# A hand-ordered RWKV-7 recurrence: triangle stores in pieces from another queue, triangle loads from ScalarE, and norm and key copies at other places

## The chip, the cores and the metric

The kernel runs on one core of one Trainium2 chip. The metric is the device time of one execution in microseconds (us). The time of before is the median of three runs, 2522.64 us (2521.0 to 2528.43). The engines are PE (TensorE), DVE (VectorE), ACT (ScalarE), POOL (GpSimd) and SP (SyncE). SP only issues DMAs here; ACT issues DMAs too, in line with its own work: a DMA instruction that has to wait for something holds up whatever stands behind it on its engine.

## The reference

A two-layer trunk of width 1024: sliding-window attention, then RWKV-7 time mixing, for a prompt of 16 meta tokens and 2048 tokens, and for a sample of 8 sequences of 4 tokens. The change lies in the second layer's recurrence. For each of 16 heads a 64x64 state S is carried over the tokens:

```
def step(S, inp):
    r_t, w_t, k_t, v_t, a_t, b_t = inp
    sa = jnp.einsum('bhvk,bhk->bhv', S, a_t)
    S = S * w_t[:, :, None, :] + sa[..., None] * b_t[:, :, None, :] + v_t[..., None] * k_t[:, :, None, :]
    return S, jnp.einsum('bhvk,bhk->bhv', S, r_t)
```

After it y is normalised per head (mean and variance over 64), scaled and shifted by ln_g and ln_b, gets a bonus in v, is multiplied by a SiLU gate, projected by w_out and added to h; a last RMS norm gives the output.

## The kernel before

**Units and chunks.** The recurrence is the last phase, from about 1600 us to the end. It goes through units one after the other: unit 0 (meta tokens), units 1 to 16 (128 prompt tokens each, in four chunks of 32), and the sample. Within a chunk the 32 steps are solved at once. `chain` (L1417 on) writes a chunk: PE forms the right-hand side `C<-Z,L`, ACT copies it (`R0s<-C`), PE multiplies by the inverse of a triangular matrix (`C<-R0s,TT`), ACT copies the result into Z (`Z<-C`, four instructions), PE forms the state (`C<-Z,LS`), and DVE writes it into the next chunk's Z (`Z<-C,pe`, four). This chain is serial from chunk to chunk and from unit to unit.

**The triangles.** TT comes from work two units ahead. `scores` (called for the two halves of a unit) lets PE form `pz<-L,BK`, from which ACT copies the triangles into `LAs` (four instructions per half) and DVE masks the rest into L. `inverse` writes `LAs` to DRAM as `la_d` (two DMAs of 128 KB, by ACT, once both halves are there), loads that back in another layout as `LA` (two DMAs of 256 KB, by SP), multiplies it on POOL by `ln` (`LA<-LA,ln`), runs 31 elimination steps of two POOL instructions each (`XT<-LA,X` and `X<-X,XT`, on a tile X that starts as the constant `laneid`), multiplies by ln (`X<-X,ln`), and stores X as `tt_d` (SP, two DMAs). `load_TT` loads that as TT (SP, two DMAs), one unit before it is used. X and LA have two buffers each. `inverse` is a generator: where it yields, the caller puts other work in between.

**Beside it.** `keys` transposes BK on PE (`kt`), and ACT copies the result into LS in groups of four. `group_norm` is the norm of the previous unit: mean and variance on DVE (`mean<-Y`, `ytm<-Y,mean`, `var<-Y` from the squares `Y<-ytm` that ACT writes), a power on POOL (`var<-var,mhalf`), then `ytm<-ytm,var`, `,lng`, `,lnb` and `,vt` on DVE; the gate multiplies (`gt<-gt,pd`, `gt<-gt,ytm`), PE transposes it (`yps<-ident,gt`). The projections `pd<-wg,xg` and `po<-wo,yp` of earlier units are cut into pieces that fill PE while the chain waits.

**What sets the order.** For units 2 to 14, `steady` writes out by hand, chunk by chunk (`ch` 0 to 3), what stands where in each engine's queue. `run(norm)` advances the group norm to its end, `run(norm, to=MARK)` to its next mark, `next(...)` one yield; work inside `released()` is placed behind the chain's last instructions on each engine. `in_order()` pins the queues of DVE, ACT and POOL. PRE is 3: the first units are prepared before the steady part. `dma(out, in, s_)` issues from ACT, without the third argument from SP. A DMA signals one of eight semaphores, in turn, and waits for the DMA eight before to land.

Of the kernel before, what the change touches and what calls it, by code (L numbers as in the profile page):

```python
# [30 lines left out]
def tile_hybrid_step(ctx: ExitStack, tc: tile.TileContext, a, o, c):  # L31
# [877 lines left out]
    def load_vectors(u):  # L909

        u.BK, u.L = [], []
        if u.kind != "p":
            room = wl.tile([P, 2, 2 * KC * 64], F32, name="rooml", tag="L", bufs=nbuf["L"])
            u.spare = room[:, 1, 512:768].rearrange("p (g v) -> p g v", v=64)
            u.BKs = room[:, 1, 0:512].rearrange("p (h g c x) -> p h g c x", h=2, g=4, c=1)
        for half in range(2):
            hs = slice(half * 4, half * 4 + 4)
            BK = es.tile([P, 4, 4, 64], F32, name="BK", tag="BK", bufs=nbuf["BK"]) if u.kind == "p" else u.BKs[:, half]
            dma(BK, bk_d[u.blk][:, hs, u.c0:u.c0 + u.nch, :])
            u.BK.append(BK)  # L920
        for c2 in range(u.np):
            if u.kind == "p":
                L = wl.tile([P, 2, 2, KC, 64], F32, name="L", tag="L", bufs=nbuf["L"])
            else:
                L = room[:, 0].rearrange("p (e c g x) -> p e c g x", e=2, c=1, g=KC)
            u.L.append(L)
            w, c0 = min(2, u.nch - 2 * c2), u.c0 + 2 * c2
            for e, ps_ in HS:

                dma(L[ps_, e].rearrange("p c g x -> p (c g x)"), ar_d[u.blk][ps_, c0:c0 + w].rearrange("p c g x -> p (c g x)"))  # L930
            yield 0.8

    us = [begin(i, *x) for i, x in enumerate(units[:-1])]
# [14 lines left out]
    def scores(u, c2):  # L948
# [22 lines left out]
        for e in range(2):  # L971
            for cc in range(w):
                r0 = 64 * cc
                tt(v_, L[OS[e], e, cc], pss[e][r0:r0 + 64], mk[r0:r0 + 64, None, :].broadcast_to([64, KC, 64]), ALU.mult)

    def inverse(u, room=None, ln=None):

        nch = u.nch
        nl = nch * 16
        la_d = dramr.tile([2, nl // 2, 32, 32], F32, name="la_d", tag=f"la_d{nch}")  # L980
        u.tt_d = tt_d = dramr.tile([32, 4, 4 * nch * 32], F32, name="tt_d", tag=f"tt_d{nch}")
        for e in range(2):
            dma(la_d[e].rearrange("l j i -> j l i"),
                u.LAs[32 * e:32 * e + 32].rearrange("p h c g i -> p (h c g) i"), s_)
        yield
        eng = v_ if u.idx == 1 else g_
        if u.kind == "m":
            room = wl.tile([P, 2, 32 * 32], F32, name="roomm", tag="L", bufs=nbuf["L"])
        if room is not None:
            LA = room[:, 0].rearrange("p (j i) -> p j i", i=32)  # L990
            XX = room[:, 1].rearrange("p (a k i) -> p a k i", a=2, i=32)
        else:

            LA = wk.tile([P, 32, 32], F32, name="LA", tag="LA", bufs=2)
            XX = None
        if XX is None:
            X = wk.tile([P, 16, 32], F32, name="X", tag="X", bufs=2)
            XT = wk.tile([P, 16, 32], F32, name="XT", tag="XT")
        else:
            X, XT = XX[:, 0], XX[:, 1]  # L1000
        if ln is None:
            ln = wp.tile([P, 32], F32, name="ln", tag=("mu", "rst0")[u.idx % 2])
        if nch < 4:
            g_.memset(LA, 0.0)
            g_.memset(ln, 1.0)
        for hh in range(2):
            dma(LA[hh * 64:hh * 64 + nl], la_d.rearrange("e l j i -> (e l) j i"), s_ if u.idx < PRE else None)
            dma(ln[hh * 64:hh * 64 + nl], ln_d[u.idx].rearrange("q c g i -> (q c g) i"))
        tt(eng, LA, LA, ln.unsqueeze(2).broadcast_to([P, 32, 32]), ALU.mult)
        dma(X, c["laneid"])  # L1010

        low = 16 if u.kind == "m" else 0

        part = {2: 16}.get(u.idx, 0)
        cut = [(v_, 0, part), (g_, part, 16)] if 0 < part < 16 else [(v_, 0, 16)] if part else [(eng, 0, 16)]
        for j in range(low, 31):
            if j in (8, 16, 22, 26):
                yield
            w = 3 - j % 4 if u.kind == "s" else 31 - j
            for eng, k0, k1 in cut if w else ():  # L1020
                ks = slice(max(low // 2, k0), min(j // 2 + 1, k1))
                shape = [P, ks.stop - ks.start, w]
                if shape[1] <= 0:
                    continue
                tt(eng, XT[:, ks, :w], LA[:, j:j + 1, j + 1:j + 1 + w].broadcast_to(shape), X[:, ks, j:j + 1].broadcast_to(shape), ALU.mult)
                tt(eng, X[:, ks, j + 1:j + 1 + w], X[:, ks, j + 1:j + 1 + w], XT[:, ks, :w], ALU.add)
        for eng, k0, k1 in reversed(cut):
            u.inverted = tt(eng, X[:, k0:k1], X[:, k0:k1], ln[:, None, :].broadcast_to([P, k1 - k0, 32]), ALU.mult)
        for hh in range(2):
            dma(tt_d[hh:32:2].rearrange("k q (l i) -> (q l) k i", i=32), X[hh * 64:hh * 64 + nl])  # L1030
# [11 lines left out]
    with ExitStack() as ph:  # L1042
# [144 lines left out]
        for x, b in enumerate(order):  # L1187
# [39 lines left out]
            if follow is None:  # L1227

                if delay:
                    todo.append((b, prv))  # L1230
                    rest_v = rest_values()
                    fill(rest_v, V0)
                wrx.close()
                es = wrx.enter_context(tc.tile_pool(name="es", bufs=1, side="right", reuse_waits="tile"))
                wl = wrx.enter_context(tc.tile_pool(name="wl", bufs=1, side="right", reuse_waits="tile"))
                for u in us[:PRE]:
                    for _ in load_vectors(u):
                        pass
                if nblk > 2:
                    banks = lambda u: [pd.tile([P, KC, 64], F32, name="pz", tag="pd") for _ in range(2)]  # L1240
                    las = wk.tile([P, 2048], F32, name="las", tag="dx", bufs=1)
                    room1 = wk.tile([P, 2, 1024], F32, name="room1", tag="xn", bufs=1)
                    for i, x0, room in ((1, 0, room1), (0, 1024, None)):
                        u = us[i]
                        u.LAs = las[:64, x0:x0 + 256 * u.nch].rearrange("p (h c g i) -> p h c g i", h=2, g=4, i=32)
                        for c2 in range(u.np):
                            all_of(scores(u, c2))
                        for _ in inverse(u, room, las[:, x0 + 1024 - 32:x0 + 1024] if i == 0 else las[:, 1536:1568]):
                            pass
            if follow is not None:  # L1250
# [18 lines left out]
    with ExitStack() as ph:  # L1269
# [71 lines left out]
        def elementwise(u):  # L1341
            load = idle() if u.L else load_vectors(u)
            next(load, None)
            small_loads(u)
            if u.tt_d is None:
                new_LAs(u)
                for c2 in range(u.np):
                    all_of(scores(u, c2))
                    next(load, None)
                    yield 0.8  # L1350
                for _ in inverse(u):
                    pass
            load_TT(u)
            yield 0.8
# [22 lines left out]
        def keys(u, c2):  # L1377
# [13 lines left out]
            for half, ps in enumerate(pss):  # L1391
                hs = slice(half * 4, half * 4 + 4)
                for cc in range(w):
                    for e in range(2):
                        act(u.LS[c2][cc][OS[e], e, hs, :], ps[cc * 64:cc * 64 + 64, :, e, :])

        def solve(u, ch, Z, R0s, out):

# [371 lines left out]
        def steady(i, u, pe):  # L1770
# [9 lines left out]
            for ch in range(4):  # L1780
# [4 lines left out]

                left = rests[::-1]
                del rests[:]
                if ch == 3:
                    run(norm)
                with released():  # L1790
                    if ch == 2:
                        next(inv.get(i + 1, idle()), None)
# [19 lines left out]
                        run(gen)  # L1812
                if ch == 2:
                    with released():
                        inv[s.idx] = inverse(s)
                        next(inv[s.idx])
                        all_of(sc)
                run(pe[ch], 1.2)
                next(rec)
                with released():  # L1820
                    if ch == 0:
# [2 lines left out]
                        first = L0s.pop(s.idx, None)  # L1824
                        load_BK(s)
                        s.L.append(first or load_L(s, 0))
                        all_of(kt)
                    if ch == 3:
                        all_of(kt)
                        next(inv[s.idx])  # L1830
                    else:
                        next(inv.get(i + 1, idle()), None)
                if ch < 2:
                    run(norm, to=MARK)
                elif ch == 3:
                    run(norms_[u.idx], to=MARK)
                run(pe[ch], 1.9)
                next(rec, None)
                with released():
# [3 lines left out]
                    if ch == 2 and i + 1 in inv:  # L1843
                        load_TT(us[i + 1])
                if ch == 2:
                    norms_[u.idx] = group_norm(u)
                    run(norms_[u.idx], to=MARK)
                    if ch == 3 and i + 3 < len(us):
# [4 lines left out]
                if ch == 1:  # L1853
                    with released():
                        new_LAs(s)
                        all_of(scores(s, 0))
                rests.append(pe[ch])
                for part in PLAN.get((i, ch), ()):
                    with released():
# [214 lines left out]
```

## Time and profile before

| | |
|---|---|
| median of the runs (2521.0, 2522.64, 2528.43) | 2522.64 us |
| the profiled execution's own time | 2526.93 us |
| its span | 2525.2 us |
| granted clock, mean over the span | 0.958 |
| busy: PE, DVE, ACT, POOL | 2238.5, 1666.3, 1169.9, 1035.9 us |
| instructions | 60868 |

The profiled execution is one run; its numbers are compared with its own time, 2526.93. In groups of instructions, the columns are busy us, the mean duration in ns, then the idle time of the engine just ahead of that group and what ended it. In a timeline a row is start, duration, engine, operation and tiles, and in brackets the idle time ahead and its releaser. Rows with an engine name ending in q (SPq, ACTq) are DMA issues: their duration is the issue, not the transfer. In the chain of waits a row that begins with DMA gives the time from issue to landing.

### The profile page before, as it was taken

What the parts mean: (1) busy time and instruction counts of PE and PEld (TensorE: products, weight loads), DVE (VectorE), ACT (ScalarE), POOL (GpSimd) and SP (SyncE); (2) the same over time, 40 slices, a digit from 0 to 9 for tenths busy, and PEclk for the clock granted to TensorE, in tenths of its full rate; (3) what the DMA queues carried; (4) which work ended last, traced back from release to release, by engine and by line L of the source; (5) the groups of instructions that cost most, each with busy time, mean ns of one, the idle gap of its engine ahead of it and who ended that gap; (6) DMA issues with size and microseconds to landing.
All of it is one profiled execution on the core that took longest, in us unless ns stands there. A gap on an engine that the chain in (4) does not pass through costs nothing. (4 is left out here: it accounts for less than half of the span.)

```text
span 2525.2 us, 60868 instructions
## 1 busy us (share of the span) xinstructions
PE 2238.5 (89%) x24932; PEld 1539.7 (61%) x24932; DVE 1666.3 (66%) x3181; ACT 1169.9 (46%) x2799; POOL 1035.9 (41%) x1572
## 2 busy tenths in 40 slices
PE   6989989899989897899999999666898888888897
PEld 5877768677855445577776668444555555555553
DVE  6586674577656987866556656555666666666674
ACT  6675465566432433554343444333444444445431
POOL 4242132333111334543333334314776766767613
PEclk9999999999999998899999999777999999999998
DMA  9433122333247564432222222575555655655323
GB/s 207 126 105 108 64 80 80 112 99 100 98 130 224 198 223 164 138 85 89 96 85 93 98 81 92 162 199 156 130 122 143 147 122 143 144 130 155 94 61 75
DMA packets 346234, 312.98 MB, mean 124 GB/s; under 512 B 205546, under 2 KB 282218, under 8 KB 344131
## 3 DMA queue, kind: packets, MB, share of 16 engines
q1 hardware_dynamic: 302515, 286.15, 38.4%
q10 hardware_dynamic: 41824, 19.15, 3.6%
q0 software_dynamic: 1616, 3.79, 0.7%
q8 instruction: 196, 3.21, 0.5%
q14 instruction: 83, 0.68, 0.1%
HBM read 191.15 MB, written 119.84 MB: 123 GB/s over the span
## 5 line engine op out<-in xcount | busy, mean ns | idle before, releaser
L38 PEld LDWEIGHTS <-yp 128*128 128x128 f16 x1488 | 141.4, 99 | 166.5 <-issue 13.4
L47 DVE SCALAR_TENSOR_TENSOR xm<-dx,mu,xn 128x256 f32<-128x256 f32 (+2 forms) x432 | 199.6, 521 | 48.4 <-POOL dx L44 47.1
L44 POOL TENSOR_TENSOR X<-X,XT 128x126 f32<-128x126 f32 (+24 forms) x458 | 186.1, 406 | 35.7
L44 POOL TENSOR_TENSOR XT<-LA,X 128x126 f32<-128x126 f32 (+24 forms) x458 | 179.7, 392 | 40.4 <-issue 6.7
L38 PE MATMUL pd<-xp,wq 128*128 128x256 f16 (+2 forms) x1728 | 186.7, 267 | 10.4 <-DVE qp L47 8.0
L38 PE MATMUL pd<-wg,xg 128*128 128x512 f16 (+1 forms) x816 | 193.5, 385 | 0.0
L38 PE MATMUL po<-wo,yp 128*128 128x512 f16 x768 | 191.3, 392 | 0.0
L38 PE MATMUL pd<-wvv,xpr 128*128 128x512 f16 (+1 forms) x816 | 189.1, 389 | 0.0
L38 PE MATMUL pd<-xpr,w 128*128 128x256 f16 (+2 forms) x1728 | 186.3, 267 | 0.0
L38 PE MATMUL pd<-xp,wg 128*128 128x256 f16 (+2 forms) x1728 | 181.9, 266 | 1.3 <-DVE xp L44 0.9
L38 PEld LDWEIGHTS <-wq 128*128 128x128 f16 x1728 | 159.5, 99 | 32.9 <-DVE qp L47 9.5
L38 PE MATMUL pd<-xpr,wkk 128*128 128x256 f16 (+2 forms) x1728 | 179.5, 264 | 0.0
L44 POOL TENSOR_TENSOR ssb<-ssb,bias 128x512 f32<-128x512 f32 x64 | 86.3, 1354 | 225.9 <-DVE ssb L462 185.4
L38 PEld LDWEIGHTS <-w 128*128 128x128 f16 x1728 | 157.8, 99 | 27.1 <-issue 9.7
L38 PEld LDWEIGHTS <-wg 128*128 128x128 f16 x1728 | 158.8, 99 | 21.7 <-issue 4.5
L38 PEld LDWEIGHTS <-wkk 128*128 128x128 f16 x1728 | 158.2, 98 | 15.6 <-issue 0.4
L38 PE MATMUL pd<-w,yp 128*128 128x512 f16 x720 | 162.3, 383 | 4.4 <-DMA yp<-y 4.4
L44 POOL TENSOR_TENSOR ps<-wst,ps 128x1024 f16<-128x1024 f32 x32 | 69.4, 2169 | 219.6 <-ACT wst L41 195.7
L44 DVE TENSOR_TENSOR Z<-C,pe 64x256 f32<-64x256 f32 x256 | 108.0, 422 | 61.0 <-PE C L38 42.9
L38 PEld LDWEIGHTS <-xpr 128*128 128x128 f16 (+1 forms) x816 | 79.2, 100 | 103.0 <-issue 18.3
L44 DVE TENSOR_TENSOR xpr<-xm,xpr 128x512 f16<-128x512 f32 (+2 forms) x144 | 98.9, 708 | 56.9 <-ACT xpr L41 56.6
L41 ACT ACTIVATE ssb<-ssb,ng 128x128 f32<-128x128 f32 (+1 forms) x272 | 104.2, 384 | 58.5 <-DVE es L44 54.8
(357 smaller groups left out, 4686.0 us busy)
## 6 DMA issues: line engine op xcount, KB each, us to landing
wst<-in_rwkv_w_in SPq DMA_DIRECT2D x32, 512.0 KB
wsp<-ps SPq DMA_DIRECT2D x32, 512.0 KB
BK<-bk SPq DMA_DIRECT2D x32, 512.0 KB
x<-in_x_prompt SPq DMA_DIRECT2D x29, 512.0 KB
xn<-xn SPq DMA_DIRECT2D x14, 1028.0 KB
ar<-aro SPq DMA_DIRECT2D x28, 512.0 KB
bk<-bko SPq DMA_DIRECT2D x28, 512.0 KB
L<-ar SPq DMA_DIRECT2D x38, 256.0 KB
```

The source lines that it names most:

```text
L38: return t_.matmul(out=out, lhsT=lhsT, rhs=rhs, start=start, stop=stop, **kw).ins
L41: return s_.activation(out=out, in_=in_, func=func, **kw).ins
L44: return e.tensor_tensor(out=out, in0=in0, in1=in1, op=op).ins
L47: v_.scalar_tensor_tensor(out=out, in0=in0, scalar=scalar, in1=in1, op0=op0, op1=op1)
```

## The change

Six edits, all in the recurrence:

1. **The stores of la_d** are cut by half-unit and by head group into eight DMAs of 32 KB a unit (`lanes_out`). Four are issued after the first half's scores (chunk 1), four after the second half's (chunk 2). For units 4 and up of the prompt (`inner`) SP issues them, else ACT.
2. **The loads of LA** of these units are issued by ACT, behind the Z copies of chunk 2, not by SP behind the previous unit's `tt_d`. The loads of ln and X stay with SP; in the code they now come ahead of LA's.
3. **The norm's last part** (`ytm<-ytm,vt`) runs at the end of chunk 2, no longer at the start of chunk 3.
4. **The key copies** of chunk 0 come in two halves, the second behind the squares of the norm.
5. **Unit 2:** the product `LA<-LA,ln` goes from POOL to DVE, where its steps were already ("third unit" in the change's words).
6. **Unit 3:** its L loads wait for the issue of its BK load.

```
         for c2 in range(u.np):
+            if u.idx == PRE:
+                hold.enter_context(tc.issue_after(last))
...
+    def lanes_out(u, parts):
+        nl = u.nch * 16
+        if 0 in parts:
+            u.la_d = dramr.tile([2, nl // 2, 32, 32], F32, name="la_d", tag=f"la_d{u.nch}")
+        for c2 in parts:
+            w = min(2, u.nch - 2 * c2)
+            for e in range(2):
+                for h in range(2):
+                    l0 = (h * u.nch + 2 * c2) * 4
+                    dma(u.la_d[e, l0:l0 + 4 * w].rearrange("l j i -> j l i"),
+                        u.LAs[32 * e:32 * e + 32, h, 2 * c2:2 * c2 + w].rearrange("p c g i -> p (c g) i"), None if inner(u) else s_)
+    def inner(u):
+        return PRE < u.idx and u.kind == "p"
...
-        for e in range(2):
-            dma(la_d[e].rearrange("l j i -> j l i"),
-                u.LAs[32 * e:32 * e + 32].rearrange("p h c g i -> p (h c g) i"), s_)
-        yield
-        eng = v_ if u.idx == 1 else g_
+        eng = v_ if u.idx in (1, 2) else g_
...
-            dma(LA[hh * 64:hh * 64 + nl], la_d.rearrange("e l j i -> (e l) j i"), s_ if u.idx < PRE else None)
             dma(ln[hh * 64:hh * 64 + nl], ln_d[u.idx].rearrange("q c g i -> (q c g) i"))
+        dma(X, c["laneid"])
+        yield
+        for hh in range(2):
+            dma(LA[hh * 64:hh * 64 + nl], la_d.rearrange("e l j i -> (e l) j i"), s_ if inner(u) or u.idx < PRE else None)
+        if inner(u):
+            yield
         tt(eng, LA, LA, ln.unsqueeze(2).broadcast_to([P, 32, 32]), ALU.mult)
-        dma(X, c["laneid"])
...
                         act(u.LS[c2][cc][OS[e], e, hs, :], ps[cc * 64:cc * 64 + 64, :, e, :])
+                yield
...
-                if ch == 3:
-                    run(norm)
...
                 if ch == 2:
                     with released():
+                        lanes_out(s, (1,))
                         inv[s.idx] = inverse(s)
...
-                        all_of(kt)
+                        next(kt, None)
...
+                    if ch == 2 and s.idx > PRE:
+                        next(inv[s.idx])
                 if ch < 2:
                     run(norm, to=MARK)
+                if ch == 0:
+                    with released():
+                        all_of(kt)
...
                 if ch == 2:
+                    run(norm)
                     norms_[u.idx] = group_norm(u)
...
-                        all_of(scores(s, 0))
+                        sc = scores(s, 0)
+                        next(sc)
+                        lanes_out(s, (0,))
+                        all_of(sc)
```

Where instructions stand now. First SP's queue in one unit of the steady part, from the loads of the unit's small data to the next output, before:

```order
L50 DMA BK<-bk_149 128x4x256 x2
L50 DMA bont<-bo_210 128x16
L50 DMA L<-ar_159 64x1024 x2
L50 DMA tt_d<-X 64x16x32 x2
L50 DMA ln<-ln_192 64x32 x2
L50 DMA LA<-la_d 64x1024 x2
L50 DMA TT<-tt_d 64x1x512 x2
L50 DMA X<-c_laneid 128x512
L50 DMA vt<-v_109 128x512 x2
L50 DMA out_y_prompt<-h_24847 128x1024
```

And the same place now:

```order
L50 DMA BK<-bk_149 128x4x256 x2
L50 DMA bont<-bo_210 128x16
L50 DMA la_d<-LAs 32x8x32 x4
L50 DMA L<-ar_159 64x1024 x2
L50 DMA la_d<-LAs 32x8x32 x4
L50 DMA tt_d<-X 64x16x32 x2
L50 DMA ln<-ln_192 64x32 x2
L50 DMA TT<-tt_d 64x1x512 x2
L50 DMA vt<-v_109 128x512 x2
L50 DMA out_y_prompt<-h_24909 128x1024
```

The eight stores came in on both sides of the L load, ahead of tt_d; the two LA loads between ln and TT went out, and X's load now stands behind the output.

Second ACT's queue in the same unit, from chunk 1's solve over chunk 2's to the gate (and, further on, chunk 0 of the next unit with the key copies LS and the squares Y), before:

```order
L41 ACTIVATE LAs<-pz 32x2x128 x4
L50 DMA la_d<-LAs 32x32x32 x2
L41 ACTIVATE Z_19047<-C 32x256 x4
L41 ACTIVATE gt<-pd 128x512
L41 ACTIVATE R0s<-C 128x256
...
L41 ACTIVATE LS_19032<-kt 64x256 x2
L41 ACTIVATE LS_19035<-kt 64x256 x2
L41 ACTIVATE LS_19032<-kt 64x256 x2
L41 ACTIVATE LS_19035<-kt 64x256 x2
L41 ACTIVATE Y_25157<-ytm 128x512
L41 ACTIVATE Y_25506<-ytm 128x512
```

And now:

```order
L41 ACTIVATE LAs<-pz 32x2x128 x4
L41 ACTIVATE Z_19055<-C 32x256 x4
L50 DMA LA<-la_d 64x1024 x2
L41 ACTIVATE gt<-pd 128x512
L41 ACTIVATE R0s<-C 128x256
...
L41 ACTIVATE LS_19040<-kt 64x256 x2
L41 ACTIVATE LS_19043<-kt 64x256 x2
L41 ACTIVATE Y_25224<-ytm 128x512
L41 ACTIVATE Y_25574<-ytm 128x512
L41 ACTIVATE LS_19040<-kt 64x256 x2
L41 ACTIVATE LS_19043<-kt 64x256 x2
```

The stores ahead of Z<-C are gone, the LA loads stand behind it, ahead of gt and R0s; the squares moved ahead of four of the eight key copies.

Third DVE's queue where chunk 2 ends and chunk 3 begins (the numbers are those of buffers), as the difference:

```order
-L44 TENSOR_TENSOR Z_19044<-C,pe 64x256 x4
-L47 SCALAR_TENSOR_TENSOR gt<-gt,pd 128x512
+L44 TENSOR_TENSOR Z_19052<-C,pe 64x256 x4
 L44 TENSOR_TENSOR ytm<-ytm,vt 128x512 x2
...
+L47 SCALAR_TENSOR_TENSOR gt<-gt,pd 128x512
+L44 TENSOR_TENSOR gt<-gt,ytm 128x512
+L47 SCALAR_TENSOR_TENSOR h_26317<-h_26317,ms_26628,fg 128x1024
```

The two ytm<-ytm,vt, which stood behind the gate's first instruction, now stand ahead of it. PE's queue keeps its order in the steady part, and POOL's changes only in unit 2's product and a few neighbours near the end.

More of the change, by code (lines that the diff above doesn't have):

```diff
@@ L915, in load_vectors @@
             u.BKs = room[:, 1, 0:512].rearrange("p (h g c x) -> p h g c x", h=2, g=4, c=1)
+        hold = ExitStack()
         for half in range(2):
@@ L918, in load_vectors @@
             BK = es.tile([P, 4, 4, 64], F32, name="BK", tag="BK", bufs=nbuf["BK"]) if u.kind == "p" else u.BKs[:, half]
-            dma(BK, bk_d[u.blk][:, hs, u.c0:u.c0 + u.nch, :])
+            last = dma(BK, bk_d[u.blk][:, hs, u.c0:u.c0 + u.nch, :])
             u.BK.append(BK)
         for c2 in range(u.np):
+            if u.idx == PRE:
+                hold.enter_context(tc.issue_after(last))
             if u.kind == "p":
@@ L930, in load_vectors @@
                 dma(L[ps_, e].rearrange("p c g x -> p (c g x)"), ar_d[u.blk][ps_, c0:c0 + w].rearrange("p c g x -> p (c g x)"))
+            hold.close()
             yield 0.8
@@ L979, in inverse @@
         nl = nch * 16
-        la_d = dramr.tile([2, nl // 2, 32, 32], F32, name="la_d", tag=f"la_d{nch}")
+        la_d = u.la_d
         u.tt_d = tt_d = dramr.tile([32, 4, 4 * nch * 32], F32, name="tt_d", tag=f"tt_d{nch}")
-        for e in range(2):
-            dma(la_d[e].rearrange("l j i -> j l i"),
-                u.LAs[32 * e:32 * e + 32].rearrange("p h c g i -> p (h c g) i"), s_)
-        yield
-        eng = v_ if u.idx == 1 else g_
+        eng = v_ if u.idx in (1, 2) else g_
         if u.kind == "m":
@@ L1247, in tile_hybrid_step @@
                             all_of(scores(u, c2))
+                        lanes_out(u, range(u.np))
                         for _ in inverse(u, room, las[:, x0 + 1024 - 32:x0 + 1024] if i == 0 else las[:, 1536:1568]):
@@ L1348, in elementwise @@
                     all_of(scores(u, c2))
+                    lanes_out(u, (c2,))
                     next(load, None)
```

## The prediction

> **What bounds the kernel now.** I read the page's chain that ended last first. It is led not by PE, the busiest engine, but by POOL:
>
> ```profile
> POOL 12%; PE 7%; DMA 5%; issue 3%; SPq 2%; DVE 1%; ACT 1%; ACTq 0%; POOLq 0%; DVEq 0%
> ```
>
> Then I followed the chain (start, duration) through one unit of the recurrence, and asked the timeline of PE for the places where the same wait ends ten units apart:
>
> ```profile
> 2033.78 4.40 DMA tt_d<-X
> ...
> 2130.74 4.16 DMA LA<-la_d
> 2135.07 1.91 POOL LA L44
> ...
> 2178.70 9.28 DMA TT<-tt_d
> ```
>
> ```profile
> 1814.34 1.06 PE L38 MATMUL C<-R0s,TT 32*32 32x64 f32 x28 [2.15 <-DMA TT<-tt_d]
> ...
> 2280.46 0.64 PE L38 MATMUL C<-R0s,TT 32*32 32x64 f32 x28 [1.92 <-DMA TT<-tt_d]
> ```
>
> From 1814.34+1.06 to 2280.46+0.64 lie ten units: 465.7 us, 46.57 each. In each, PE waits for TT, which was stored (tt_d) after POOL's last X, whose unit POOL could only begin when LA had been loaded, which SP issues behind that same store of the unit before. So the period is a loop of POOL, SP and DMA: POOL ends X at 2125.42+1.26 = 2126.68, gets LA 8.38 later, and works to 2172.79:
>
> ```profile
> 2125.42 1.26 POOL L44 TENSOR_TENSOR X<-X,ln 128x512 f32<-128x512 f32 x1
> 2135.06 1.91 POOL L44 TENSOR_TENSOR LA<-LA,ln 128x1024 f32<-128x1024 f32 x1 [8.38 <-DMA Z<-v]
> ...
> 2151.61 0.20 POOL L1623 TENSOR_SCALAR var<-var 128x16 f32<-128x16 f32 x1
> ...
> 2155.28 1.33 POOL L44 TENSOR_TENSOR X<-X,XT 128x135 f32<-128x135 f32 x1
> ...
> 2158.54 0.42 POOL L44 TENSOR_TENSOR XT<-LA,X 128x130 f32<-128x130 f32 x1
> ...
> 2171.52 1.27 POOL L44 TENSOR_TENSOR X<-X,ln 128x512 f32<-128x512 f32 x1
> ```
>
> ```profile
> 2126.71 1.34 SPq L50 DMA_DIRECT2D tt_d<-X  x2
> 2128.10 1.33 SPq L50 DMA_DIRECT2D ln<-ln  x2
> 2129.54 1.80 SPq L50 DMA_DIRECT2D LA<-la_d  x2
> 2131.53 1.09 SPq L50 DMA_DIRECT2D TT<-tt_d  x2
> ```
>
> (The releaser named on POOL's row, Z<-v, merely landed last; the chain shows LA.) How close PE stands behind this loop, the groups of those ten units show (busy, mean ns, idle before):
>
> ```profile
> L38 PE MATMUL C<-R0s,TT 32*32 32x64 f32 x1281 | 32.0, 222 | 21.4 <-DMA TT<-tt_d 21.3
> L38 PE MATMUL C<-Z,LS 128*64 128x64 f32 x1280 | 56.5, 228 | 10.9 <-ACT Z L41 8.2
> L38 PE MATMUL C<-Z,L 128*32 128x64 f32 x1280 | 26.2, 222 | 12.1 <-issue 9.2 <-PE po L38 2.1 <-DMA Z<-v 0.7
> L1676 PE MATMUL yps<-ident,gt 128*128 128x128 f32 x81 | 15.2, 315 | 11.5 <-DVE gt L44 11.5
> L44 POOL TENSOR_TENSOR LA<-LA,ln 128x1024 f32<-128x1024 f32 x10 | 19.1, 1912 | 86.0 <-DMA Z<-v 77.2 <-DMA LA<-la_d 8.8
> ```
>
> ```profile
> 1815.40:2281.10 465.70, 409.40 (x7602) 247.34 (x7602) 311.24 (x500) 213.40 (x540) 326.13 (x690) 0.98 0.58 138
> ```
>
> The last gives the stretch, then busy us of PE, PEld, DVE, ACT, POOL. PE is busy 409.40 of 465.70, so 40.9 per unit is its floor. POOL idles 8.6 before LA, but PE has only 2.13 of TT wait to give back.
>
> **The change part by part.**
>
> *LA from ScalarE, la_d in eight pieces from SP.* POOL no longer waits for its own last store. Its next halt is var, the group norm's variance, which DVE makes from the squares that ScalarE writes:
>
> ```profile
> 2127.65 0.69 DVE L47 SCALAR_TENSOR_TENSOR gt<-gt,pd 128x512 f32<-128x512 f32 x1 [1.74 <-ACT gt L41]
> 2128.26 1.28 DVE L44 TENSOR_TENSOR ytm<-ytm,vt 128x512 f32<-128x512 f32 x2
> 2129.58 0.69 DVE L44 TENSOR_TENSOR gt<-gt,ytm 128x512 f32<-128x512 f32 x1
> 2130.18 1.28 DVE L47 SCALAR_TENSOR_TENSOR h<-h,ms,fg 128x1024 f32<-128x1024 f32 x1
> ...
> 2149.51 1.29 DVE L1620 TENSOR_REDUCE var<-Y 128x8 f32<-128x512 f32 x2 [2.99 <-ACT Y L41]
> ...
> 2156.32 1.38 DVE L44 TENSOR_TENSOR ytm<-ytm,lng 128x1024 f32<-128x1024 f32 x1
> ```
>
> ```profile
> 2141.21 0.64 PE L38 MATMUL C<-R0s,TT 32*32 32x64 f32 x28 [2.16 <-DMA TT<-tt_d]
> ...
> 2152.66 0.65 PE L38 MATMUL C<-Z,L 128*32 128x64 f32 x32 [1.04 <-issue]
> ...
> 2169.47 1.87 PE L38 MATMUL C<-Z,LS 128*64 128x64 f32 x32 [0.60 <-ACT Z L41]
> ```
>
> DVE's var is ready at 2150.80 and POOL takes it at 2151.61: only 0.81 of slack. So with LA early, POOL would stop there, and the loop becomes: PE's solve begins (2141.21), var 9.59 later, POOL from var to the last X 2172.79−2151.61 = 21.18, then X to the next solve. That last leg is now 2141.21−2126.68 = 14.53 (ten of them mean about 14.9, from 46.57 − 9.59 − 0.81 − 21.18 = 14.99). Without LA's issue (1.80) ahead of it TT can go up to 2.0 sooner, but TT must also wait until tt_d has landed, which took 4.40 in the chain's row; and it shares the queues with LA no longer. Bounds: 0.5 to 2.2 gained; I take 1.3, nearer the SP row, so 13.7.
>
> *The squares ahead of the second half of the key copies.*
>
> ```profile
> 2148.89 1.10 ACT L41 ACTIVATE Y<-ytm 128x512 f32<-128x512 f32 x2
> ...
> 2166.49 1.54 ACT L41 ACTIVATE LAs<-pz 32x256 f32<-32x256 f32 x4 [2.31 <-PE pz L38]
> 2168.06 0.94 ACTq L50 DMA_DIRECT2D la_d<-LAs  x2
> 2169.05 1.56 ACT L41 ACTIVATE Z<-C 32x256 f32<-32x256 f32 x4 [1.02 <-issue]
> 2173.43 0.60 ACT L41 ACTIVATE gt<-pd 128x512 f32<-128x512 f32 x1 [2.82 <-PE pd L38]
> ```
>
> Four copies of about 0.38 (1.54 / 4, the like-sized LAs) go behind the squares, so var is ready 1.5 sooner: 9.59 − 1.5 = 8.1. That also frees DVE for Z<-C, which PE's C<-Z,L awaits: its issue wait, 9.2 / 10 = 0.92, should go. The delayed copies are read chunks later, so they cost nothing.
>
> *The norm's last step ahead of gt.* DVE idles 1.74 before gt<-gt,pd; ytm<-ytm,vt (1.28) fits there, so PE's wait for gt, 11.5 / 10 = 1.15, goes.
>
> *No la_d issue on ScalarE ahead of Z<-C.* This frees up to 1.02; PE's wait behind it is 8.2 / 10 = 0.82, of which I take 0.6, one row's wait. What comes instead: the LA load stands behind Z<-C and waits until all eight pieces have landed, and gt and R0s queue behind it. gt is wanted 2173.43 − 2168.03 = 5.4 after the last LAs copy, 4.4 once Z moves up by 1.0. The last piece is issued within about 1 of that copy; its landing is bounded by tt_d's 4.40 above and about 2 below (an estimate: 9.28 for TT of four times a piece's size, divided by four); the issue adds 0.9 (half of 1.80) to 1.8. So ScalarE comes free 3.9 to 7.2 after the copy: nothing, or up to 2.8 per unit. I take 0.
>
> Row against rule: one 128 KB la_d issue cost ScalarE 0.94 / 2 = 0.47, so four pieces for two should cost SP about 1 more in idle time. The Trainium skill, "DMA: Bandwidth & Descriptors", Rules for kernel authors, says to coalesce many small transfers, and that under 64 KB one pays mostly overhead; pieces of 32 KB break that. By it the change would lose where ScalarE waits for the last piece, and the sum would be the slower rival's 2555 below; no row here shows a 32 KB la_d store.
>
> *New loops.* PE alone: 46.57 − 2.13 − 0.92 − 1.15 − 0.6 = 41.8. Through var: 8.1 + 0.2 (hand-over, an estimate from the gaps of 0.1 to 0.3 between POOL's rows) + 21.2 + 13.7 = 43.2. Through LA: the last LAs copy comes 2168.03−2141.21−0.92 = 25.9 after the solve began, LA lands some 8 to 10 later (piece 3 to 5, issue 1, load 4.16), POOL needs 2172.79−2135.06 = 37.7, the last leg 13.7; over two periods, 85.3 to 87.3, 42.7 to 43.7 each. POOL's early steps now also run beside DVE's two-input operations: one X step took 1.33 at 2155.28 beside ytm, its like 0.42 at 2158.54. If the 3.25 of ytm, gt and h (1.28 + 0.69 + 1.28) all collide, this loop gets 1.6 longer, 45.3 at most. The Trainium skill, "GPSIMD Engine Reference", Specifications, says that POOL shares its SBUF interfaces with VectorE, with contention where the latter has two SBUF inputs; the row agrees, and by it the collision is to be expected whole, and the sum is that of the third rival below.
>
> *The ends.* Units 1 to 3: LA·ln of unit 2 goes from POOL to DVE (1.91 by POOL's row) beside unit 2's steps, which DVE does already; bounds ±2. The hold of unit 3's L loads until the BK issue: ±2. In unit 2 the first SP pieces stand behind TT's load, and ScalarE behind them, as it stood 3.29 for TT before:
>
> ```profile
> 1746.16 3.21 ACTq L50 DMA_DIRECT2D la_d<-LAs  x2
> 1749.41 1.56 ACT L41 ACTIVATE Z<-C 32x256 f32<-32x256 f32 x4 [3.29 <-DMA TT<-tt_d]
> ```
>
> I take +4 there, against the same savings as elsewhere in units 2 and 3 (2 × 3.4), and something like one period's for the units after 2281: together −2 to −6, I take −2.
>
> **Sum.** 43.2 for 46.57 saves 3.37 a unit, 33.7 over ten, 35.7 with the ends. The profiled execution took 2526.93 (span 2525.2), 4.3 above the median 2522.64; so 2491.2 for it, and **2487** for the median.
>
> **The rivals.** (The measurement tells 0.3%, 7.6 us, from no change.)
>
> - *Forecast*, var's loop at 42.5 to 44.2: (46.57−42.5)×10 + 2 = 42.7 down to 25.7 saved, 2480 to 2497. Chance 0.55. For it: var's 0.81 of slack and the closed PE waits, each a row.
> - *PE-bound*, 41.8: TT comes before it is wanted, if the last leg is 12.3 or less (8.1+0.2+21.2+12.3). Saves 47.7 + 2, 2473. Against it: TT's own 9.28. Chance 0.12.
> - *Half kept*: LA late, POOL slowed beside DVE, or gt held by 1 to 2 on ScalarE: 44.2 to 45.5, say 45.0: saves 17.7, 2505. Chance 0.20.
> - *The waits only change place* (the loop through DMA as long as before): within 7.6 us, about 2521. Chance 0.05. The change that isn't what it says falls here: LA behind a ScalarE queue that is never free sooner.
> - *Slower*: the LA load holds ScalarE in every unit. The small pieces land late, each 9.28 after its issue as TT does, so ScalarE is free 1 + 9.3 + 0.9 = 11.2 after the last copy, where gt is wanted at 4.4: 6.8 held, 3.4 more than saved: 34 over ten units, 2 off at the ends, 2555. It decides from a landing of 5.9 after the issue (4.4 + 3.4 − 0.9 − 1). Against it: tt_d, a store too, took 4.40. Chance 0.08.
>
> Range 2470 to 2508: it takes in the first three, 0.87, less what stands over at the third's far end. Faster 0.87, same 0.05, slower 0.08.
>
> **What would show it.** Right: in the same ten units PE's waits for gt and for Z on C<-Z,L near nothing; POOL's wait of 8.6 for LA shrinks to 4 to 6 (LA lands 34 to 36 after the solve began, the last X ends 29.5 after it), with 0 to 1 at var behind it; PE's wait for TT 1 to 2; period 43.2. Wrong: ScalarE's gt or R0s waits for an LA load (slower rival); POOL waits at LA for over 6.5 (half kept); no wait for TT at all (PE-bound). A time above 2515 means that the loop was not POOL's.

## The result, and the profile after

The changed kernel takes 2512.88 us (median of 8 runs, 2506.91 to 2519.06) against 2524.48 for before (8 runs, 2521.0 to 2529.14): a ratio of 0.9948, interval 0.9936 to 0.9961. It is faster, by 0.5%, where 1.4% was forecast; the time lies 5 us above the range. The profiled execution has a span of 2511.8 (before: 2525.2), so 13.4 us to account for. (Below, one of the four runs of e8_both took 12270 us, five times the others, and is left out of its median.)

PE's first solve of a unit (the end of `C<-R0s,TT` in chunk 0) marks the places; the ten units from unit 4 to unit 14 give the period, the time of one unit. Here are the rows for the ends of the stretch that the prediction used, and for unit 1, after the change:

```profile
1658.58 1.07 PE L38 MATMUL C<-R0s,TT 32*32 32x64 f32 x32 [2.65 <-ACT R0s L41]
...
1823.42 0.65 PE L38 MATMUL C<-R0s,TT 32*32 32x64 f32 x32
...
2270.56 0.65 PE L38 MATMUL C<-R0s,TT 32*32 32x64 f32 x32
```

And unit 1 before:

```profile
1654.83 1.06 PE L38 MATMUL C<-R0s,TT 32*32 32x64 f32 x28 [3.96 <-DMA TT<-tt_d]
```

| stretch | before | after | saved |
|---|---|---|---|
| to unit 1's first solve | 1655.9 | 1659.65 | -3.8 |
| unit 1 to unit 4 | 159.5 | 164.4 | -4.9 |
| unit 4 to unit 14, ten units | 465.7 | 447.1 | 18.6 |
| from there to the end | 244.1 | 240.6 | 3.5 |

So the period fell from 46.57 to 44.71, not to 43.2, and the stretches ahead of unit 4 lost 8.7, where the sum had 4 lost against 6.8 saved. Of the 35.7 us forecast 15.1 are missing in the ten units and 7.2 at the two ends. The groups of the ten units, in the same columns as before, and the busy times of the engines:

```profile
L38 PE MATMUL C<-Z,LS 128*64 128x64 f32 x1280 | 58.5, 228 | 12.0 <-ACT Z L41 8.2
...
L38 PE MATMUL C<-R0s,TT 32*32 32x64 f32 x1281 | 31.6, 222 | 17.7 <-DMA TT<-tt_d 17.0 <-ACT R0s L41 0.4
...
L38 PE MATMUL C<-Z,L 128*32 128x64 f32 x1280 | 26.2, 222 | 1.2 <-PE po L38 1.2
...
L44 POOL TENSOR_TENSOR LA<-LA,ln 128x1024 f32<-128x1024 f32 x10 | 19.3, 1928 | 49.6 <-DMA LA<-la_d 49.6
L1701 PE MATMUL yps<-ident,gt 128*128 128x128 f32 x80 | 14.4, 307 | 4.5 <-DVE gt L44 4.5
...
L1648 POOL TENSOR_SCALAR var<-var 128x16 f32<-128x16 f32 x10 | 2.0, 204 | 16.1 <-DVE var L1645 15.9
```

```profile
1824.07:2271.21 447.14, 411.46 (x7601) 246.91 (x7600) 315.44 (x501) 211.93 (x540) 327.72 (x686) 0.97 0.60 144
```

PE's wait ahead of C<-Z,L is gone (9.2 of issue to none), gt's fell from 11.5 to 4.5, POOL's for LA from 86.0 to 49.6. But PE still waits 17.0 for TT, and POOL now waits 15.9 for var. One unit, POOL first:

```profile
2027.19 1.27 POOL L44 TENSOR_TENSOR X<-X,ln 128x512 f32<-128x512 f32 x1
...
2032.21 1.91 POOL L44 TENSOR_TENSOR LA<-LA,ln 128x1024 f32<-128x1024 f32 x1 [3.75 <-DMA LA<-la_d]
...
2051.54 0.20 POOL L1648 TENSOR_SCALAR var<-var 128x16 f32<-128x16 f32 x1 [3.00 <-DVE var L1645]
...
2072.14 1.27 POOL L44 TENSOR_TENSOR X<-X,ln 128x512 f32<-128x512 f32 x1
```

Then the chain of waits through the same unit, whose DMA rows run from issue to landing:

```profile
2029.16 5.57 DMA tt_d<-X
...
2035.35 8.14 DMA TT<-tt_d
```

And the queues of SP and ACT there:

```profile
2028.48 1.35 SPq L50 DMA_DIRECT2D tt_d<-X  x2
2029.88 3.60 SPq L50 DMA_DIRECT2D ln<-ln  x2
2034.78 1.09 SPq L50 DMA_DIRECT2D TT<-tt_d  x2
```

```profile
2027.23 1.10 ACTq L50 DMA_DIRECT2D LA<-la_d  x2
2028.38 0.60 ACT L41 ACTIVATE gt<-pd 128x512 f32<-128x512 f32 x1 [2.95 <-PE pd L38]
...
2028.95 5.39 ACTq L50 DMA_DIRECT2D Z<-v  x2
2034.38 0.60 ACT L41 ACTIVATE yp<-yps 128x512 f16<-128x512 f32 x1 [5.08 <-DMA tt_d<-X]
```

POOL's last X ends at 2028.46. tt_d is issued at once, but the LA load went out 1.2 us earlier on ACT, and tt_d lands at 2029.16 + 5.57 = 2034.73, 6.3 after X's end. SP has LA no longer in its way, yet TT can be issued only then, at 2034.78, and lands at 2043.49: 15.0 after X, as before the change. ACT too waits for tt_d: its Z<-v load reuses the semaphore of a DMA eight before, tt_d, and holds yp until it has landed.

### The profile page after: what moved, and what is told of

The parts are those of the page before. It is cut to its first block, busy times and chain, and to the rows that moved or that the text cites. A ratio compares the mean times of both kernels' runs of the same rounds, so it can differ in the third digit from the quotient of the medians.

```text
span 2511.8 us, 61024 instructions
## 1 busy us (share of the span) xinstructions
PE 2247.4 (89%) x24932; PEld 1544.0 (61%) x24932; DVE 1674.6 (67%) x3182; ACT 1169.3 (47%) x2799; POOL 1032.5 (41%) x1571
## 4 chain that ended last, share of the span: by engine, by line
PE 33%; DVE 20%; DMA 14%; POOL 14%; ACT 10%; issue 6%; SPq 3%; ACTq 0%; POOLq 0%; DVEq 0%
PE pd L38 23%; POOL X L44 4%; DVE xm L47 4%; POOL XT L44 3%; SPq L50 3%; DVE xpr L44 2%; DMA tt_d<-X 2%; DMA TT<-tt_d 2%; ACT ssb L41 2%; PE po L38 2%; POOL var L44 1%; PE sc L38 1%; PE C L38 1%; DMA wst<-in_rwkv_w_in 1%; DMA vt<-v 1%
## 5 line engine op out<-in xcount | busy, mean ns | idle before, releaser
L38 PE MATMUL pd<-wg,xg 128*128 128x512 f16 (+1 forms) x816 | 200.4, 395 | 0.0
L44 POOL TENSOR_TENSOR XT<-LA,X 128x126 f32<-128x126 f32 (+24 forms) x458 | 181.0, 395 | 46.3 <-DMA wo<-wsp 12.7
L38 PEld LDWEIGHTS <-xg 128*128 128x128 f16 (+1 forms) x816 | 77.1, 101 | 90.4 <-issue 13.3
L44 DVE TENSOR_TENSOR xpr<-xm,xpr 128x512 f16<-128x512 f32 (+2 forms) x144 | 98.9, 709 | 50.0 <-ACT xpr L41 49.6
```

The costliest lines, as they stand in the source:

```text
L38: return t_.matmul(out=out, lhsT=lhsT, rhs=rhs, start=start, stop=stop, **kw).ins
L44: return e.tensor_tensor(out=out, in0=in0, in1=in1, op=op).ins
```

## The experiments

The ends of the first solves, read from PE's timeline in each profile, show where each version gains. The first column scatters among executions of one and the same kernel (1654.4 and 1645.8 for e8 and e11, the same kernel), so the start is judged by the stretch from unit 1 to 4, and by the medians of the runs.

| kernel | unit 1 | unit 4 | 1 to 4 | per unit, 4 to 14 | median | ratio to before (interval) |
|---|---|---|---|---|---|---|
| before | 1655.9 | 1815.4 | 159.5 | 46.57 | 2524.5 | |
| after | 1659.7 | 1824.1 | 164.4 | 44.71 | 2512.9 | 0.9948 (0.9936 to 0.9961) |
| e1_whole_start | 1657.6 | 1812.4 | 154.8 | 45.14 | 2504.4 | 0.9903 (0.9868 to 0.9938) |
| e2_keys_back | 1660.5 | 1824.4 | 163.9 | 46.37 | 2526.1 | 0.9994 (0.9977 to 1.0011) |
| e3_early_la | 1664.0 | 1827.2 | 163.2 | 44.21 | 2506.8 | 0.9905 (0.9887 to 0.9923) |
| e4_tt_four | 1655.2 | 1806.8 | 151.6 | 41.79 | 2471.9 | 0.9768 (0.9747 to 0.9789) |
| e5_la_on_sp | 1664.3 | 1828.4 | 164.0 | 45.41 | 2526.4 | 0.9995 (0.9980 to 1.0010) |
| e6_norm_back | 1654.8 | 1817.4 | 162.5 | 44.45 | 2516.7 | 0.9976 (0.9958 to 0.9995) |
| e7_before_tt_four | 1654.9 | 1802.6 | 147.8 | 46.62 | 2508.2 | 0.9938 (0.9920 to 0.9956) |
| e9_unit2_pool | 1654.0 | 1796.0 | 141.9 | 42.24 | 2459.4 | 0.9747 (0.9711 to 0.9783) |
| e10_no_hold | 1659.5 | 1806.2 | 146.7 | 42.00 | 2455.8 | 0.9723 (0.9698 to 0.9748) |
| e8_both | 1654.4 | 1797.6 | 143.1 | 42.70 | 2459.8 | 0.9756 (0.9727 to 0.9784) |
| e11_both_again (same) | 1645.8 | 1788.3 | 142.5 | 42.37 | 2460.3 | 0.9729 (0.9705 to 0.9754) |
| e12_tt_four_again (as e4) | 1662.7 | 1817.9 | 155.2 | 41.91 | 2473.1 | 0.9786 (0.9762 to 0.9811) |

**Is the loop through var the one that sets the period?** Two versions, one that lengthens it and one that shortens it at another place. The first puts the key copies back:

```
-                        next(kt, None)
+                        all_of(kt)
                     if ch == 3:
```

> The changed kernel with all eight key copies of chunk 0 ahead of the squares again. Theory that the loop through var sets the period (last X, tt_d, TT, solve, var, last X): var is 1.5 us later in every unit, the period goes from 44.7 to about 46.2, the time up by 15 to 17 us, to about 2529. Rival (the loop is POOL's wait for LA, 3.5 to 6.5 us a unit, and var has slack): the time moves by less than 4 us, though PE's wait ahead of C<-Z,L comes back by 0.9 us a unit.

The period went to 46.37 (1.66 longer), the time to 2526.1, 13 more. PE's wait came back and POOL's wait for var grew from 15.9 to 34.3:

```profile
L38 PE MATMUL C<-Z,L 128*32 128x64 f32 x1280 | 26.2, 222 | 16.2 <-issue 13.4 <-PE po L38 1.7 <-DMA Z<-v 1.2
...
L1648 POOL TENSOR_SCALAR var<-var 128x16 f32<-128x16 f32 x10 | 2.0, 203 | 34.3 <-DVE var L1645 34.3
```

The rival, POOL's wait for LA, falls: POOL stands still for var 3.4 us a unit, and the delay of the key copies (1.5 by the forecast) moved the period by 1.66. The second version deals TT's load out anew; TT's source is walked as 2 x 32 rows of 2 KB, now as 32 rows at a time:

```
             for gh in range(2):
-                dma(u.TT[64 * gh:64 * gh + 64].rearrange("p c g i -> p (c g i)"), u.tt_d[:, gh:4:2].rearrange("k q x -> q k x"))
+                for q in range(2):
+                    p0 = 64 * gh + 32 * q
+                    dma(u.TT[p0:p0 + 32].rearrange("p c g i -> p (c g i)"), u.tt_d[:, gh + 2 * q])
```

> The changed kernel with TT loaded by four DMAs of 32 partitions in place of two of 64 (whose two-level rows, the trace shows, signal from few DMA engines). Theory that the last leg sets the period: if each piece is spread over all engines, TT lands 3.5 to 5 us after its issue and not 8 to 9, the leg falls from 14.9 to about 10.5, PE no longer waits for TT, the period falls to 42 (PE's own chain), the time by 22 to 28 us, to about 2487. Rival (TT's landing is set by the traffic beside it, not by its shape): the leg falls by less than 1 us, the time by less than 8.

2471.9, 41 less than the changed kernel: more than expected. The period is 41.79, where the prediction had put PE's own chain at 41.8. The groups of its ten units and SP's queue in one of them:

```profile
L38 PE MATMUL C<-R0s,TT 32*32 32x64 f32 x1281 | 28.5, 218 | 2.3 <-DMA TT<-tt_d 1.8 <-ACT R0s L41 0.4
...
L1650 POOL TENSOR_SCALAR var<-var 128x16 f32<-128x16 f32 x10 | 2.0, 203 | 1.4 <-DVE var L1647 0.6
```

```profile
1806.79:2224.70 417.91, 396.88 (x7601) 240.66 (x7600) 316.87 (x501) 212.39 (x540) 328.97 (x684) 1.00 0.63 155
```

```profile
2001.17 1.34 SPq L50 DMA_DIRECT2D tt_d<-X  x2
2002.56 3.02 SPq L50 DMA_DIRECT2D ln<-ln  x2
2006.86 1.72 SPq L50 DMA_DIRECT2D TT<-tt_d  x4
```

PE waits 1.8 for TT in ten units, where it waited 17.0, and is busy 396.88 of 417.91. In this unit (X ends at 2001.14) the four pieces land 1.9 to 2.1 after their issue and the last at 2010.20, 9.1 after X; over the ten units the leg is 8.9 on average, against 14.9. Most of the rest is the start: unit 1 to unit 4 takes 151.6 and not 164.4, and PE's wait for TT ahead of unit 2's first solve falls from 16.5 to 12.7; besides, the front of this profile was 4.5 ahead.

The Trainium skill, "DMA: Bandwidth & Descriptors", section "Why a DMA increments its semaphore by 16 and not by 1", has the rule: the number of DMA engines is the largest one up to 16 that divides the slowest dimension of both access patterns. By it the old load, whose source begins with a dimension of 2, goes to two engines, and the new one, with 32, to sixteen. The trace agrees: the semaphore of each old load is written 3 times, that of each new one 16 times, as for tt_d, and the times to landing are 8.14 for the second of two 128 KB loads and about 2.0 for each of four of 64 KB. The same page's "Rules for kernel authors", which the prediction weighed, says to coalesce small transfers; here halving the transfers won, since the spread counted for more.

**Was TT in the loop before the change?** The same four loads in the kernel before, and nothing else:

> The kernel before the change, with TT loaded by four DMAs of 32 partitions and nothing else changed. Theory that the old loop ran through POOL, tt_d and LA alone: TT comes some 6 us sooner but POOL's wait for LA keeps the period at 46.1 to 46.6; only the start (PE's waits of 10 us for TT in units 1 and 2) gains, 3 to 8 us in all, about 2519. Rival (TT sat in the loop of before too): the period falls to 43 or less, the time by 30 us or more.

The period is 46.62, where it was 46.57; TT's wait is gone and PE waits elsewhere, while POOL waits for LA as ever:

```profile
L38 PE MATMUL C<-R0s,TT 32*32 32x64 f32 x1281 | 28.2, 218 | 0.0
...
L44 POOL TENSOR_TENSOR LA<-LA,ln 128x1024 f32<-128x1024 f32 x10 | 19.1, 1912 | 84.4 <-DMA LA<-la_d 75.8 <-DMA Z<-v 8.6
```

So the prediction's reading of the loop of before was right, and the change did break it: a faster TT is worth nothing per unit before and 2.9 per unit after. Its gain of 16 to 17 us there is more than the 3 to 8 expected; in the profile 11.7 of it lie in units 1 to 4 (159.5 to 147.8) and 3.3 behind unit 14.

**What the move of LA did to the leg.** First LA back in SP's queue, behind tt_d:

```
-            dma(LA[hh * 64:hh * 64 + nl], la_d.rearrange("e l j i -> (e l) j i"), s_ if inner(u) or u.idx < PRE else None)
+            dma(LA[hh * 64:hh * 64 + nl], la_d.rearrange("e l j i -> (e l) j i"), s_ if u.idx < PRE else None)
```

> The changed kernel with the LA loads of units 4 and up issued by SyncE again, behind tt_d (and ahead of ln). Theory that the move to ScalarE is what broke the old loop: POOL gets LA about 7.2 us after its last X (tt_d's issue 1.3, LA's 1.8, landing 4.2), so a unit takes 7.2 + 16.5 + 21.8 = 45.5 us against 44.7; 11 units, plus 8 to 10 us, about 2522. Rival (LA's queue is of no account, the gain came from the re-placed norm and key copies): within 3 us of the changed kernel's 2513.

45.41 per unit and 2526.4: the old loop is back, POOL waits 6.5 for LA in the unit below and for var in none of the ten. The period explains 7.0 of the 13.5 us lost, and 3.1 more lie behind unit 14; the rest stays open. But the leg became shorter, 13.2 on average, although LA's two issues stand ahead of TT's again:

```profile
2039.37 1.35 SPq L50 DMA_DIRECT2D tt_d<-X  x2
2040.89 1.20 SPq L50 DMA_DIRECT2D LA<-la_d  x2
2042.14 0.60 SPq L50 DMA_DIRECT2D ln<-ln  x1
2042.83 1.09 SPq L50 DMA_DIRECT2D TT<-tt_d  x2
```

tt_d, now issued 1.5 ahead of LA, lets TT be issued 3.5 after its own issue (2042.83 against 2039.37), where with LA on ACT it took 6.3 (2034.78 against 2028.48); over the ten units tt_d lands 3.9 after X on average, against 6.2. The second test loads the same bytes earlier, from the half of la_d that is stored first (half the lanes' triangles are left out):

```
                         lanes_out(s, (0,))
+                        if inner(s):
+                            s.early = wk.tile([P, 32, 32], F32, name="LA", tag="LA", bufs=2)
+                            for p0 in range(0, P, 32):
+                                dma(s.early[p0:p0 + 32].rearrange("p j i -> p (j i)"),
+                                    s.la_d.rearrange("e (h y) j i -> (e h) y (j i)", h=2)[:, 0:8])
                         all_of(sc)
```

> The changed kernel, but for units 4 and up LA is loaded by SyncE right after the first four pieces of la_d, from those pieces alone, each taken twice: the triangles of half the lanes are left out, the bytes loaded are the same, and the load is over before POOL's last X. Theory that the LA load, issued within 0.5 us of tt_d, slows tt_d's landing (5 to 6.5 us after X's end, 3 to 5 in the kernel before) and so keeps the leg from X's end to TT at 14.9 us: tt_d lands after 3 to 4 us, the leg falls to about 13, POOL's wait for LA is gone, the period is 42.5 to 43.2, the time about 2494. Rival (the leg is long for TT's own transfer, whatever runs beside it): the leg stays above 14.4 and the time falls by 5 us at most.

The leg is 14.5, the period 44.21, the time 6 us less: by the letter the rival's outcome. But the load was not over before X, as the test needed: in the trace its first piece was issued 3 to 6 us ahead of X's end and its last landed 2.5 to 5.5 after it, so it still ran beside tt_d, and POOL's wait for LA did not go either (30.9 in ten units). These pieces begin with a dimension of 4, and the semaphore of each is written 5 times: they landed 4.0 to 6.6 after issue for 128 KB, where ACT's loads of 256 KB take 3.3 to 5.7. The run doesn't separate the two theories.

The other traces do, as the place of LA's issue varies by itself. In one unit of e4, ACT's row first, then SP's:

```profile
2165.13 1.10 ACTq L50 DMA_DIRECT2D LA<-la_d  x2
```

```profile
2170.89 1.34 SPq L50 DMA_DIRECT2D tt_d<-X  x2
...
2174.30 2.10 SPq L50 DMA_DIRECT2D TT<-tt_d  x4
```

LA is issued 5.7 ahead of X's end (2170.86), and TT can be issued 3.4 after tt_d. Ten versions load LA from ACT in this place (the changed kernel, e1, e2, e4, e6 and e8 to e12), which makes a hundred units. In eight of them LA is issued more than 5.5 ahead of X's end, and tt_d lands 3.3 to 3.4 after it each time; in 57 it is issued up to 1.5 ahead, and tt_d lands 5.5 to 7.0 after; the units with LA 1.5 to 5 ahead lie between (3.5 to 5.6), and those with LA behind X's end scatter (3.5 to 7.4). So LA beside tt_d lengthens tt_d, as e5 shows from the other side, though no run moved LA's issue and nothing else; e4 shows that the larger part of the leg is TT's own shape.

**The start.** Whole la_d stores up to unit 3, from ACT as before the change:

```
             u.la_d = dramr.tile([2, nl // 2, 32, 32], F32, name="la_d", tag=f"la_d{u.nch}")
+        if not inner(u):
+            if u.np - 1 in parts:
+                for e in range(2):
+                    dma(u.la_d[e].rearrange("l j i -> j l i"),
+                        u.LAs[32 * e:32 * e + 32].rearrange("p h c g i -> p (h c g) i"), s_)
+            return
```

> The changed kernel, but units up to 3 store la_d again as two whole DMAs from ScalarE; units 4 and up keep the eight pieces from SyncE. Start theory: the eight pieces of unit 2, six of them waiting for earlier DMAs, held ScalarE for 8.8 us in unit 1 and made everything behind late; unit 4's first solve, 8.7 us later than in the kernel before, comes back to within 3 us of it, the period of units 4 to 14 stays 44.7 us, and the time falls by 6 to 8 us, to about 2505. Rival (unit 2's product on VectorE, and its tt_d behind the weight loads in SyncE's queue, cost the start): the time falls by 2 us at most.

The time fell by 8.5, the stretch from unit 1 to 4 by 9.6, to 154.8, less than before the change. ACT's queue in unit 1, after the change and with the whole stores:

```profile
1649.31 8.78 ACTq L50 DMA_DIRECT2D la_d<-LAs  x6
1658.14 0.38 ACT L41 ACTIVATE R0s<-C 128x256 f32<-128x256 f32 x1 [9.50 <-DMA la_d<-LAs]
```

```profile
1648.78 0.38 ACT L41 ACTIVATE R0s<-C 128x256 f32<-128x256 f32 x1 [1.74 <-PE C L38]
1648.86 1.22 ACTq L50 DMA_DIRECT2D la_d<-LAs  x2
```

Six pieces took 8.78 to issue, since some of them had to wait for the landing of the DMA eight before, and R0s, which PE needs, stood behind them for 9.50. (With the whole stores the order on ACT also has R0s ahead of them; the two were not tried apart.) The four runs, 2497.0 to 2516.1, overlap those of the changed kernel, so the median alone is weak evidence; the pair on one chip below is better. The period did not stay at 44.7 as expected but was 45.14; with the four loads, too, it is longer with the whole stores (42.70 and 42.37 against 41.79 and 41.91), which no run explains.

**The norm's place.** The norm's last part back at the start of chunk 3:

```
+                if ch == 3:
+                    run(norm)
                 with released():
...
                 if ch == 2:
-                    run(norm)
                     norms_[u.idx] = group_norm(u)
```

> The changed kernel with the norm's last part at the start of chunk 3 again. Theory that the loop through TT and var sets the period: PE's wait for gt comes back with 1.15 us in each unit, and the wait for TT (about 2.4) shrinks by as much; the time moves by 3 us at most. Rival (PE's own chain sets the period as well): plus 1.15 us in 11 units, about 12 us, 2525.

The median, 2516.7, is 3.8 above the changed kernel's; the two intervals overlap. Per unit nothing was lost (44.45). The wait moved as expected, from TT to gt:

```profile
L38 PE MATMUL C<-R0s,TT 32*32 32x64 f32 x1281 | 31.5, 222 | 14.0 <-DMA TT<-tt_d 13.1 <-ACT R0s L41 0.8
...
L1701 PE MATMUL yps<-ident,gt 128*128 128x128 f32 x81 | 14.4, 302 | 15.9 <-DVE gt L44 15.8
```

**Both repairs together,** and, on one chip, once more both and the four loads alone:

> The changed kernel with both repairs: whole la_d stores from ScalarE up to unit 3, and TT loaded by four DMAs. Theory that start and loop are separate places: the gains add, 8 us from the start and 41 from the loop, about 2464. Rival (the start's loss was TT's wait seen from the other side, and the four loads had repaired it): within 2 us of 2472.

> The version with both repairs once more, in five rounds, on the same chip as the next one. Theory that start and loop are separate: 7 to 9 us under the one with TT by four DMAs alone, about 2464.

> TT by four DMAs alone once more, in five rounds: about 2472. If it comes within 3 us of the one before, the whole stores at the start give nothing once TT is fast.

2459.8 and 2460.3 with both, 2473.1 with the four loads alone: 12.8 apart on one chip, more than the 7 to 9 expected. The two places are separate. With both, the kernel takes 0.9729 of the time of before (0.9705 to 0.9754), so it beats before and after. The two small edits at the start were taken out of that version, unit 2's product first, then unit 3's hold:

```
-        eng = v_ if u.idx in (1, 2) else g_
+        eng = v_ if u.idx == 1 else g_
```

> The version with both repairs (whole la_d stores up to unit 3, TT by four DMAs), and unit 2's product LA by ln on GpSimd again. Theory that this edit was worth little: the product takes 1.23 us on VectorE and 1.9 on GpSimd, so within 3 us of the version with both repairs, 2462 to 2468. Rival (the product and the waits it adds to VectorE's queue, where the masks of unit 3 stand, were a second cause of the late start): 4 us or more faster.

```
-            if u.idx == PRE:
-                hold.enter_context(tc.issue_after(last))
```

> The version with both repairs, without the hold of unit 3's L loads. Theory that the hold only sets which of two early loads comes first: within 3 us of the version with both repairs, 2462 to 2468. Rival (the hold sends the L loads into the stretch where TT of unit 2 is stored and loaded, and costs there): 4 us or more faster.

2459.4 and 2455.8 against 2460.3: neither can be told from nothing. The second is 4.5 lower, past the rival's mark, but the two intervals overlap.

## Why the prediction was wrong

**Right.** The loop of before (POOL, tt_d, LA) and that the change breaks it: e7 and e5. That the loop through var follows it: e2. POOL's wait for LA of 4 to 6: 5.0 (the one at var behind it is 1.6, not 0 to 1). PE's wait for TT of 1 to 2: 1.7. C<-Z,L's 0.92: gone. That the LA load on ACT doesn't hold gt: in the unit shown gt waits 2.95 for PE's pd, not for the load; the small stores of la_d there land 1.6 to 3.3 after their issue, where the prediction's bounds were 2 and 4.40.

**Right by luck, PE's own chain.** 41.8 was forecast, and e4 shows 41.79. But the sum is 40.9 busy, called a floor, and 0.8 idle; e4 has 39.7 busy, at a granted clock of 1.00 where before it was 0.98, and 2.1 idle, 0.9 of it for gt.

**Wrong, the last leg.** The step "Bounds: 0.5 to 2.2 gained; I take 1.3" for the leg from X to TT. Measured over the ten units: 14.9 again, nothing gained. The prediction named tt_d's landing as the limit, but took it at 4.40, a row of a unit in which LA was issued behind tt_d. Behind "it shares the queues with LA no longer" stands the step that failed: that is true of TT, which takes 8.6 from the first issue to the landing, where it took 10.1. But LA moved from sharing with TT to sharing with tt_d, which now lands 5.4 to 7.0 after X (before: 3.3 to 5.1), so TT is issued 6.2 after X and not 4.9. The gain of one is the loss of the other. That is 1.2 of the 1.5 us per unit that are missing. The rest: var to the last X takes 21.9 in the unit shown (2051.54 to 2073.41), not 21.2, and 22.0 on average, since one or two more of POOL's steps now run slowly beside DVE (0.73 and 0.80 in the unit shown, beside vt<-vt,bont, where their like take 0.42); TT's landing to var takes 7.6, not 8.1, and the hand-over 0.3. 14.9 + 7.6 + 0.3 + 22.0 = 44.8, the measured 44.7.

**Wrong, the saving behind Z.** "PE's wait behind it is 8.2 / 10 = 0.82, of which I take 0.6". The la_d issue is gone from ACT, but C<-Z,LS still waits 8.2 in ten units: the waiting Z<-v load, held for tt_d's landing, took its place ahead of yp and Z<-C. It cost nothing while TT was later still, and it stood only in PE's own chain, not in the 43.2.

**Wrong, the start.** "I take −2" for the two ends stood against a loss of 5.2 in the profile (3.8 + 4.9 - 3.5). Edit 1 was costed for the units in which SP issues the pieces; for units 1 to 3, where ACT does, issues that wait were counted as nothing. e1 gives back 8.5 us in the median, and e11 12.8 against e12. Of the 3.8 ahead of unit 1 it stays open how much is the pieces and how much the scatter of that column.

**Not seen at all.** TT's 9.28 for 128 KB was quoted, with tt_d's 4.40 for as many bytes beside it. The question why one takes twice the other was the best one in the profile: it led to 41 us on top of the change, where all six edits gave 12.

## What to carry to other kernels

When a load is taken out of a queue, ask where its bytes will now move, not only what the queue gains: here LA, issued just ahead of the critical tt_d, made it land some 2 to 3 us later. A DMA whose time is out of line with its bytes is worth its own look, its first dimension above all: here 2 against 32 rows made 8 us against 2. Small DMAs in the queue of a computing engine can hold that engine when they wait for the landing of earlier ones: here 9.5 us.

## What the runs showed of the hardware

- In the ten units, two 128 KB loads that begin with a dimension of 2 landed 5.5 to 6.5 and 7.8 to 8.7 us after issue (after); four 64 KB loads of 32 rows 1.9 to 3.3 (e4), and 2.6 to 4.1 beside the LA loads (e7).
- tt_d, two 64-row stores in 128-byte pieces, had landed 3.3 to 5.0 us after X's end where the LA loads followed it (e5), 5.4 to 7.0 where they were issued within 1.3 us of X's end (after), and 3.3 to 3.4 where they were issued more than 5.5 ahead of it (eight units of e4, e8, e10 and e12).
- The granted clock in the ten units was 1.00 with the four loads (e4; 0.99 in e12), where PE was busy 95% of the time, and 0.97 after the change, where it was 92%: here a busier PE was not throttled more.
